# A two-block network on one core: the scan's turns, the last scores of a neighbourhood, and the preparation's products on VectorE

## The chip, the cores and the metric

The program runs on one core of one Trainium2 chip. Its time is the device time in microseconds (us) from start to end of one execution. The engines of the core are TensorE (PE in the profile, its weight loads PEld), VectorE (DVE), ScalarE (ACT), GpSimd (POOL) and SyncE (SP), whose queue issues nearly all the DMAs. Before the change the median of three runs is 4197.6 us, from 4195.8 to 4206.4. The profile was taken in a further execution, of 4200.8 us.

## The reference, cut to what matters

Two blocks follow one another, each of two layers. The change touches the layers of the first block alone. A layer projects 256 context and 1024 latent tokens, runs a recurrence over them in both directions (six heads of 64), a full attention, and a neighbourhood attention, in which a row of 64 queries sees eight rows of keys, with a bias for each place, and all 256 context keys:

```
def _rwkv7_step(S, inp):                  # lax.scan, forwards and backwards
    r, w, k, v, kk, b = inp
    sa = einsum('bhvk,bhk->bhv', S, kk)
    S = S * w - sa[..., None] * b + v[..., None] * k
    return S, einsum('bhvk,bhk->bhv', S, r)

def row_block(r):                         # neighbourhood attention
    s_nb  = einsum('bqhd,bpqjhd->bhqpj', q_r, k_nb) + bias
    s_ctx = einsum('bqhd,bchd->bhqc', q_r, k_ctx)
    p = softmax(concatenate([s_nb, s_ctx], -1))
    return p_nb @ v_nb + p_ctx @ v_ctx
```

Here `kk` is the normalized key, `kd = k * (1 + (iclr - 1) * k_a)` stands for `k` in the step, and `b = kk * iclr`.

## The kernel before, in words

The recurrence is computed in 20 steps of 64 tokens, both directions in one step. Within a step the 64 x 64 triangular system of the recurrence is inverted, so that a step is only matmuls.

**Preparation** (`rwkv_pre`, in `project`) makes what the steps need. For each of the 20 steps `front` loads r, k and kk (`RKK`), forms the decay's running sum `L` with a scan on VectorE (line 869), its exponentials `pf` and `pinv` on ScalarE, the rates `ic` (line 866, GpSimd), `b` (line 876, GpSimd) and `kd` (lines 878 and 879, VectorE), and from these the four products of `T4` (lines 885 to 888, one of them on GpSimd). In the trace `T4` is called `T`. `back` multiplies two of the four on TensorE and stores all of them. After five steps `rwkv_solve` inverts 30 systems at once: a product into `stmp` (`dot`, line 956, in turn on GpSimd and VectorE) and a sum over it (line 958, VectorE), first row by row, then with blocks of 8 and of 16. There are four solves in a layer. All of this is a generator which `project` runs in turn with the remaining projections (`late_proj`, matmuls `pj`). A weight of the projections is split into `hhi` (ScalarE) and the rest `hlo` (`split`, line 129); `lo_engine` says which engine takes the second, and during the preparation that is GpSimd.

**The scan** (`rwkv_steps`) runs after that, in turn with the attention (`attention1`). `seqs` gives turns: the scan has weight 60, the attention 80 (`W1`), so that four turns of the attention go with three of the scan. A step takes three turns: first `rw<-SV,Z` and half of the next step's `fetch` (direction 0: `rw<-T`, masked on VectorE into `Z` and `G`), then `rw<-W,TT`, then `rw<-SV,BT` and `rw<-G,SV`. At its end the rest of `fetch` is drained at once: direction 1's `rw<-T`, and the transposes of both directions, copied to `BT` by ScalarE. The tiles `rw` have three buffers in PSUM. 

**The attention** finds the largest score of every query first (`maxima`). For each tile of 128 queries and each head scores are written to `S` (two buffers) and reduced on VectorE (line 1451). A neighbourhood tile has 512 keys with a bias (`biased`, line 1458), then 256 context keys, and for the tiles 2 to 5 of 8 another 64 keys with a bias, written into the same `S` behind the context's. After that `weights` makes T = scores transposed, exponentials `gP`, and blends `Y`.

TensorE's order is that of the code (`ordered`); a scheduler orders the other engines. Each engine runs its queue in order.

## Time and profile before

| stretch of the span (us) | what runs | length | TensorE busy | VectorE busy | GpSimd busy |
|---|---|---|---|---|---|
| 280 to 690 | preparation, first layer | 410 | 351.3 | 308.1 | 224.0 |
| 690 to 1103 | scan, first layer | 413 | 350.8 | 271.8 | 211.4 |
| 1580 to 2017 | preparation, second layer | 437 | 367.1 | 308.5 | 231.7 |
| 2017 to 2415 | scan, second layer | 398 | 352.1 | 264.8 | 206.6 |
| whole span | both blocks | 4198.9 | 3669.6 | 2750.2 | 1551.5 |

The profiled execution took 4200.8 us, of which 4198.9 are the span in the profile. The first block's scans and preparations are 1658 us of it, the four stretches of the table; the rest is the first projections of each layer, the end of its attention, the output projections and the second block. Busy times of TensorE include the time in which its clock is reduced.

### The profile page before, as it was taken

The page shows a single profiled execution, that of the slowest core. Times are in us where ns is not written, and L with a number is a line of the kernel's source. Part 1 is how long each engine was busy: PE and PEld are TensorE (multiplying, and loading weights), DVE is VectorE, ACT ScalarE, POOL GpSimd, SP SyncE. Part 2 cuts the span into 40 slices and gives each one's busy share as a digit, 9 for nine tenths or more (in the row PEclk, how much of TensorE's full clock was granted, in tenths as well). Part 3 has the DMA queues.
Part 4 walks back from the last instruction along what each step waited for, and adds up shares of the span by engine and source line. Part 5 has one row for each costly group of instructions (what it writes and reads, how often), then busy time and mean ns, then how long its engine had stood idle before and what let it go on. Part 6 is the DMA issues. An engine that isn't in the chain of part 4 may idle for free. (4 is left out here: it accounts for less than half of the span.)

```text
span 4198.9 us, 67804 instructions
## 1 busy us (share of the span) xinstructions
PE 3669.6 (87%) x25828; PEld 2732.5 (65%) x25828; DVE 2750.2 (65%) x4527; ACT 1722.4 (41%) x3354; POOL 1551.5 (37%) x1482
## 2 busy tenths in 40 slices
PE   7999887988888899887888988898889799788988
PEld 5767665655546677665555645686667687566767
DVE  4547877666787755778557677756766553676655
ACT  3235442333442225443334443235555522555551
POOL 2215653555663223556355564103111320311132
PEclk9999988999999999888899999898999999899999
DMA  6448654233334226773423234233232342322233
GB/s 241 167 116 186 156 142 129 89 100 105 120 96 157 81 80 162 169 164 98 136 88 120 82 127 148 92 123 98 67 97 81 102 141 85 103 73 93 75 107 126
DMA packets 509845, 495.75 MB, mean 118 GB/s; under 512 B 296360, under 2 KB 412616, under 8 KB 505168
## 3 DMA queue, kind: packets, MB, share of 16 engines
q1 hardware_dynamic: 469264, 455.76, 36.4%
q10 hardware_dynamic: 40256, 35.66, 2.8%
q8 instruction: 204, 3.34, 0.3%
q14 instruction: 121, 0.99, 0.1%
HBM read 323.81 MB, written 167.49 MB: 117 GB/s over the span
## 5 line engine op out<-in xcount | busy, mean ns | idle before, releaser
L107 PE MATMUL pj<-hthi,hhi 128*128 128x512 f32 (+2 forms) x2120 | 868.6, 410 | 49.7 <-DVE stg L715 31.4
L107 PE MATMUL pj<-hthi,hlo 128*128 128x512 f32 (+2 forms) x2120 | 814.3, 384 | 4.2 <-POOL hlo L129 4.2
L107 PE MATMUL pj<-htlo,hhi 128*128 128x512 f32 (+2 forms) x2120 | 814.6, 384 | 0.5 <-DVE htlo L129 0.5
L107 PEld LDWEIGHTS pj<-hthi,hhi 128*128 128x128 f32 (+1 forms) x2120 | 413.9, 195 | 158.5 <-DVE stg L715 34.0
L107 PEld LDWEIGHTS pj<-hthi,hlo 128*128 128x128 f32 (+1 forms) x2120 | 411.9, 194 | 86.1 <-POOL hlo L129 4.6
L107 PEld LDWEIGHTS pj<-htlo,hhi 128*128 128x128 f32 (+1 forms) x2120 | 414.4, 195 | 61.7 <-DVE htlo L129 1.6
L1544 POOL TENSOR_TENSOR acc<-acc,gP 128x512 f32<-128x512 f32 (+1 forms) x240 | 305.2, 1284 | 173.0 <-ACT gP L1538 155.9
L129 POOL TENSOR_TENSOR hlo<-hraw,hhi 128x1024 fp32r<-128x1024 f32 x65 | 168.9, 2599 | 251.1 <-ACT hhi L128 243.0
L1538 ACT ACTIVATE gP<-T 128x512 f32<-128x512 f32 (+1 forms) x292 | 167.1, 583 | 190.8 <-PE T L107 178.8
L1451 DVE TENSOR_REDUCE gmx<-S 128x1 f32<-128x512 f32 (+1 forms) x372 | 202.5, 555 | 60.2 <-PE S L107 58.2
L107 PE MATMUL po<-who,yh 128*128 128x512 f32 x544 | 216.7, 398 | 27.5 <-ACT yh L1658 22.6
L107 PE MATMUL S<-K,B 128*128 128x512 f32 (+2 forms) x448 | 174.3, 390 | 67.7 <-DVE gmx L1451 59.7
L107 PE MATMUL po<-wlo,yh 128*128 128x512 f32 x544 | 216.2, 397 | 0.0
L107 PE MATMUL po<-who,yl 128*128 128x512 f32 x544 | 214.1, 395 | 1.1 <-POOL yl L1659 1.1
L128 ACT CAST hhi<-hraw 128x1024 fp32r<-128x1024 f32 x118 | 123.8, 1049 | 220.9 <-PE pj L107 178.1
L1182 POOL TENSOR_SCALAR RL<-rl 128x128 f32<-128x128 f32 (+1 forms) x80 | 35.6, 446 | 467.3 <-DVE rl L1299 415.4
L107 PE MATMUL Y<-gP,V 128*64 128x512 f32 (+1 forms) x776 | 202.9, 608 | 2.0 <-DVE ys L1557 2.0
L107 PEld LDWEIGHTS S<-K,B 128*128 128x128 f32 x448 | 86.7, 193 | 153.8 <-DVE gmx L1451 108.2
L107 PE MATMUL T<-B,K 128*128 128x512 f32 (+1 forms) x368 | 167.1, 454 | 11.2 <-ACT gP L1538 9.8
L107 PE MATMUL S<-KL,L 128*128 128x512 f32 (+2 forms) x448 | 158.3, 354 | 0.0
L107 PE MATMUL T<-L,KL 128*128 128x512 f32 (+1 forms) x368 | 145.4, 396 | 2.7 <-DVE L L122 2.7
L1659 POOL TENSOR_TENSOR yl<-yr,yh 128x1024 fp32r<-128x1024 f32 x34 | 83.1, 2443 | 162.1 <-ACT yh L1658 144.9
(422 smaller groups left out, 8499.9 us busy)
## 6 DMA issues: line engine op xcount, KB each, us to landing
hraw<-in_w_in_dram SPq DMA_DIRECT2D x110, 512.0 KB
T<-d_PRE SPq DMA_DIRECT2D x40, 768.0 KB
mw<-in_w_mod_dram SPq DMA_DIRECT2D x24, 1024.0 KB
RKK<-d_U SPq DMA_DIRECT2D x80, 288.0 KB
yr<-d_YT ACTq DMA_DIRECT2D x34, 512.0 KB
d_G<-stg SPq DMA_DIRECT2D x64, 256.0 KB
woraw<-in_w_out_dram SPq DMA_DIRECT2D x32, 512.0 KB
d_PRE<-T SPq DMA_DIRECT2D x40, 384.0 KB
```

Of the source, the lines that this page charges most:

```text
L107: self.nc.tensor.matmul(out, lhsT=lhsT, rhs=rhs, start=start, stop=stop, skip_group_check=True)
L128: self.nc.scalar.copy(hi, src)
L129: self.lo_engine.tensor_tensor(out=lo, in0=src, in1=hi.bitcast(F32), op=ALU.subtract)
L1182: self.nc.gpsimd.tensor_scalar(out=out, in0=in_, scalar1=1.0, scalar2=0.0, op0=ALU.mult, op1=ALU.add)
L1451: nc.vector.tensor_reduce(out=m, in_=S[:, 0:w], op=ALU.max, axis=AX.X, negate=True)
L1538: nc.scalar.activation(P, T, AF.Exp)
L1544: eng.tensor_tensor(out=acc[h][:, cs], in0=acc[h][:, cs], in1=P, op=ALU.add)
L1659: nc.gpsimd.tensor_tensor(out=yl, in0=y, in1=yh.bitcast(F32), op=ALU.subtract)
```

## The change

Five things change. In a neighbourhood tile the scores of the last 64 keys are written together with the context's, ahead of the reduction of these; the two reductions follow. In the scan `fetch` is given out in two parts: the transposes of direction 0 (`turn(0)`) with direction 1's products in a turn of their own, `turn(1)` at the end of the step. A step then has four turns, and with weight 79 against 80 the scan and the attention alternate strictly. In the preparation GpSimd's pieces go to VectorE: `ic`, `b`, the product with r, `hlo`, and GpSimd's half of the solve's products. `b` and `kd` share a tile `BK`, so that their two products with `pinv` are one instruction. And the solve's 16-blocks leave out what a triangular block has as zeros: a product has 1024, 768, 512 and 256 columns instead of four times 1024. The sums over them shrink alike.

```diff
-                    seqs((scan, 60), att, until=scan)
+                    seqs((scan, 79), att, until=scan)
...
-                self.lo_engine = self.nc.gpsimd
...
-                nc.gpsimd.tensor_scalar(out=ic[:, d], in0=th[1][:, d, :, o:o + 64], scalar1=0.5, scalar2=0.5, op0=ALU.mult,
+                nc.vector.tensor_scalar(out=ic[:, d], in0=th[1][:, d, :, o:o + 64], scalar1=0.5, scalar2=0.5, op0=ALU.mult,
                                         op1=ALU.add)
...
-            b = t3("b")
-            nc.gpsimd.tensor_tensor(out=b, in0=ic, in1=kk, op=ALU.mult)
-            kd = t3("kd")
+            BK = self.tl(rp, [128, 2, 2, 3, 64], F32, "BK")
+            kd = BK[:, 1]
+            nc.vector.tensor_tensor(out=BK[:, 0], in0=ic, in1=kk, op=ALU.mult)
...
-                nc.gpsimd.tensor_tensor(out=T4[:, d, :, 1, :], in0=self.rev(r[:, d], d), in1=pf[:, d, :, 1:65], op=ALU.mult)
-                nc.vector.tensor_tensor(out=T4[:, d, :, 2, :], in0=self.rev(b[:, d], d), in1=pinv[:, d], op=ALU.mult)
-                nc.vector.tensor_tensor(out=T4[:, d, :, 3, :], in0=self.rev(kd[:, d], d), in1=pinv[:, d], op=ALU.mult)
+                nc.vector.tensor_tensor(out=T4[:, d, :, 1, :], in0=self.rev(r[:, d], d), in1=pf[:, d, :, 1:65], op=ALU.mult)
+                both = BK[:, :, d, :, ::-1] if d else BK[:, :, d]
+                nc.vector.tensor_tensor(out=T4[:, d, :, 2:4, :].rearrange("p a q t -> p q a t"), in0=both,
+                                        in1=pinv[:, d].unsqueeze(1).to_broadcast([128, 2, 3, 64]), op=ALU.mult)
...
-            self.turn = (self.turn + 1) % 2
-            (nc.gpsimd if self.turn else nc.vector).tensor_tensor(out=tv, in0=x.to_broadcast([128] + shape),
-                                                                  in1=y.to_broadcast([128] + shape), op=ALU.mult)
+            nc.vector.tensor_tensor(out=tv, in0=x.to_broadcast([128] + shape), in1=y.to_broadcast([128] + shape), op=ALU.mult)
...
-                    dot(X[:, i:i + step, :], blk(D, o + n, o, n)[:, i:i + step, :].unsqueeze(2), t11, [step, n, n])
+                    dot(X[:, :, i:i + step], blk(D, o + n, o, n)[:, :, i:].unsqueeze(2), t11[:, i:i + step, i:].unsqueeze(1),
+                        [n, step, n - i])
...
+            def turn(d):
+                ps = self.tl(rpp, [128, 3, 128], F32, "rw", 3)
+                for p in range(3):
+                    self.tr(ps[:, p, :], row(T4[:, d, p, 2:4, :]), self.ID)
+                nc.scalar.copy(BT[:, d], ps)
             for d in range(2):
+                if d:
+                    turn(0)
                 gp = [self.tl(rpp, [128, 3, 128], F32, "rw", 3) for _ in range(2)]
...
-            BT = self.tl(rp, [128, 2, 3, 128], F32, "BT", 2)
-            for d in range(2):
-                ps = self.tl(rpp, [128, 3, 128], F32, "rw", 3)
-                for p in range(3):
-                    self.tr(ps[:, p, :], row(T4[:, d, p, 2:4, :]), self.ID)
-                nc.scalar.copy(BT[:, d], ps)
-            yield
+            turn(1)
             return tok, AR, TT, G, Z, BT
...
             if st < 19:
+                next(ahead)
+                yield
                 ready = self.drain(ahead)
...
                 scores(S[:, 0:w], h, t, k0, w)
+                if near:
+                    scores(S[:, w:w + near[2]], h, t, *near[1:3])
                 m = mx[:, t, 1 - h, c:c + 1]
                 nc.vector.tensor_reduce(out=m, in_=S[:, 0:w], op=ALU.max, axis=AX.X, negate=True)
                 if near:
                     biased(S, w, h, t, *near)
             def biased(S, o, h, t, c, k0, w, b0):
-                scores(S[:, o:o + w], h, t, k0, w)
```

Line 107 before is line 106 after, 110 is 109, and 956 is 953. The instructions' numbers of tiles differ between the two programs.

TensorE before, in the first layer's scan where a step ends and the next begins (`T` is the step's operands, `rw` a PSUM tile, `CST` holds the identity for the transposes):

```order
L107 MATMUL T_7949<-acc_7711,ONES 64x256
L107 MATMUL rw_7959<-T_1261_7742 128x128
L107 MATMUL rw_7960<-T_1261_7742 128x128
...
L110 MATMUL rw_7972<-CST,T_1261_7742 128x128 x3
L110 MATMUL rw_7977<-CST,T_1261_7742 128x128 x3
L107 MATMUL rw_7991<-SV_7741,Z_7766 64x64 x12
L107 MATMUL rw_8008<-T_1318_7983 128x128
```

TensorE after, at the same place:

```order
L106 MATMUL T_7890<-acc_7652,ONES 64x256
L109 MATMUL rw_7900<-CST,T_1245_7698 128x128 x3
L106 MATMUL rw_7905<-T_1245_7698 128x128
L106 MATMUL rw_7906<-T_1245_7698 128x128
...
L106 MATMUL T_7917<-B_6147,K_5963 128x512
...
L106 MATMUL S_7944<-KL_6598,L_6943 128x64
L109 MATMUL rw_7955<-CST,T_1245_7698 128x128 x3
L106 MATMUL rw_7969<-SV_7697,Z_7722 64x64 x12
L106 MATMUL rw_7987<-T_1308_7961 128x128
```

The first three transposes now stand ahead of direction 1's six products, and a turn of the attention stands between these products and the last three transposes with `rw<-SV,Z`.

TensorE before, with what an instruction waits for, at the first neighbourhood tile with 64 more keys (`S` scores, first layer's scan):

```order
L107 MATMUL S_7873<-K_6656,B_7001 128x256 [waits DVE_49]
L107 MATMUL S_7873<-KL_6657,L_7002 128x256
L107 MATMUL S_7873<-K_6656,B_7001 128x64 [waits DVE_49]
L107 MATMUL S_7873<-KL_6657,L_7002 128x64
L107 MATMUL S_7881<-K_6656,B_7001 128x512
```

TensorE after, at the same tile:

```order
L106 MATMUL S_7814<-K_6597,B_6942 128x256 [waits DVE_49]
L106 MATMUL S_7814<-KL_6598,L_6943 128x256
L106 MATMUL S_7814<-K_6597,B_6942 128x64
L106 MATMUL S_7814<-KL_6598,L_6943 128x64
L106 MATMUL S_7822<-K_6597,B_6942 128x512 [waits DVE_49]
```

The wait for VectorE ahead of the 64 keys is gone, and the next tile of scores, which takes the other buffer of `S`, has one.

VectorE after, in the first layer's preparation, near the end of a solve (`BK` holds b and kd, `stmp` a product, `sX` and `sT` blocks of the inverse, `hlo` a weight's rest):

```order
L953 TENSOR_TENSOR stmp_3887<-sT_3417,sX_618_3783 128x256
L953 TENSOR_TENSOR stmp_3902<-sT_3417,sX_618_3783 128x512
L128 TENSOR_TENSOR hlo_3820<-hraw_3817,hhi_3819 128x1024
L954 TENSOR_REDUCE sT_3417<-stmp_3887 128x4x16
L954 TENSOR_REDUCE sT_3417<-stmp_3902 128x4x16
...
L874 TENSOR_TENSOR BK_4006<-ic_3995,RKK_3991 128x384
L875 SCALAR_TENSOR_TENSOR BK_4006<-ic_3995,ka_418_2562 128x384
L953 TENSOR_TENSOR stmp_3915<-sT_3417,sX_618_3783 128x768
L953 TENSOR_TENSOR stmp_3924<-sT_3417,sX_618_3783 128x1024
```

Before, `hlo`, `b` and two of these four products, each of 1024 columns, stood in GpSimd's queue; now all are in VectorE's, between the solve and the steps' own products.

## Rows read from the trace of the kernel before

**Rows 1.** Busy time by stretch: the two preparations and the two scans, with TensorE's granted clock.

```profile
280.00:690.00 410.00, 351.30 (x3005) 285.83 (x3003) 308.12 (x356) 186.12 (x462) 223.97 (x220) 0.91 0.62 150
690.00:1103.00 413.00, 350.76 (x3903) 241.68 (x3902) 271.79 (x615) 159.12 (x318) 211.36 (x224) 0.95 0.33 101
1580.00:2017.00 437.00, 367.11 (x2894) 286.04 (x2892) 308.51 (x368) 190.16 (x463) 231.70 (x214) 0.88 0.62 150
2017.00:2415.00 398.00, 352.13 (x3714) 235.29 (x3714) 264.83 (x591) 154.23 (x294) 206.59 (x211) 0.96 0.33 104
```

**Rows 2.** TensorE's waits, first preparation: us in total, times, longest us.

```profile
PE pre L107 <- ACT sXs L997: 15.7, 8, 7.1
PE pre L107 <- DVE T L887: 15.1, 2, 14.1
PE pj L107 <- DVE stg L706: 9.2, 5, 5.0
```

**Rows 3.** TensorE's longest wait in the second preparation.

```profile
PE pre L107 <- DVE sD L984: 21.4, 2, 19.4
```

**Rows 4.** TensorE's waits, first scan.

```profile
PE S L107 <- DVE gmx L1451: 27.5, 29, 7.5
PE rw L110 <- DVE G L1055: 22.5, 19, 7.1
```

**Rows 5.** TensorE's waits, second scan.

```profile
PE S L107 <- DVE gmx L1451: 18.3, 26, 2.5
PE rw L110 <- DVE G L1055: 12.8, 19, 1.9
```

**Rows 6.** TensorE's timeline: first and last of 32 waits ahead of 64 keys.

```profile
811.15 0.30 PE L107 MATMUL S<-K,B 128*128 128x64 f32 x1 [1.86 <-DVE gmx L1451]
...
2338.47 0.30 PE L107 MATMUL S<-K,B 128*128 128x64 f32 x1 [0.52 <-DVE gmx L1451]
```

**Rows 7.** TensorE's timeline: second group of transposes at the end of a step.

```profile
728.38 0.52 PE L110 MATMUL rw<-CST,T 128*128 128x128 f32 x3 [0.43 <-DVE G L1055]
```

**Rows 8.** Both preparations' busy sums: L956, L958, tiles RKK and pinv, L869, L878.

```profile
sum 847.00, DVE 131.30 POOL 151.02; mean DVE 65.65 POOL 75.51
sum 847.00, DVE 111.16; mean DVE 55.58
sum 847.00, DVE 89.42 POOL 110.17; mean DVE 44.71 POOL 55.08
sum 847.00, DVE 88.21 ACT 20.87; mean DVE 44.11 ACT 10.43
sum 847.00, DVE 54.71; mean DVE 27.35
sum 847.00, DVE 28.74; mean DVE 14.37
```

**Rows 9.** Timeline of VectorE and GpSimd in the first preparation: start, duration.

```profile
540.52 0.96 DVE L869 TENSOR_TENSOR_SCAN L<-rst,lw 128x384 f32<-128x384 f32 x1 [1.93 <-ACT lw L865]
...
555.31 0.35 DVE L885 TENSOR_TENSOR T<-RKK,pPF 128x192 f32<-128x192 f32 x1
...
564.97 2.93 POOL L956 TENSOR_TENSOR stmp<-sD,sT 128x1024 f32<-128x1024 f32 x1 [2.58 <-DVE sT L958]
565.93 2.79 DVE L869 TENSOR_TENSOR_SCAN L<-rst,lw 128x384 f32<-128x384 f32 x1
568.64 2.18 DVE L956 TENSOR_TENSOR stmp<-sD,sT 128x1024 f32<-128x1024 f32 x1
```

**Rows 10.** VectorE's longest wait for GpSimd, first preparation.

```profile
DVE L L869 <- POOL ic L866: 10.9, 1, 10.9
```

**Rows 11.** VectorE's waits for GpSimd's products, second preparation.

```profile
DVE sT L958 <- POOL stmp L956: 9.7, 10, 1.8
```

**Rows 12.** Weight splits on VectorE, whole span: busy, mean ns, idle before and releaser.

```profile
L129 DVE TENSOR_TENSOR hlo<-hraw,hhi 128x1024 fp32r<-128x1024 f32 x53 | 65.4, 1234 | 91.2 <-ACT hhi L128 90.3
```

**Rows 13.** The rates on GpSimd in the second preparation, same columns.

```profile
L866 POOL TENSOR_SCALAR ic<-th 128x192 f32<-128x192 f32 x40 | 23.9, 605 | 75.2 <-ACT th L147 53.7 <-issue 16.6 <-DVE L L869 2.6
```

More of the change, by code (lines that the diff above doesn't have):

```diff
@@ L81, in __init__ @@
         self.flip = 0
-        self.turn = 0
         self.tanhs, self.logs = [], []
@@ L563, in project @@
                     next(att)
-                self.lo_engine = self.nc.vector
                 while self.flow:
@@ L973, in rwkv_solve @@
                 X = self.tl(rp, [128, n, n], F32, f"sX{n}", 2 if n == 8 else 1)
-                t11 = blk(T, o, o, n).rearrange("p j k -> p k j").unsqueeze(1)
+                t11 = blk(T, o, o, n).rearrange("p j k -> p k j")
                 for i in range(0, n, step):
-                    dot(X[:, i:i + step, :], blk(D, o + n, o, n)[:, i:i + step, :].unsqueeze(2), t11, [step, n, n])
+                    dot(X[:, :, i:i + step], blk(D, o + n, o, n)[:, :, i:].unsqueeze(2), t11[:, i:i + step, i:].unsqueeze(1),
+                        [n, step, n - i])
                     yield
-                xv = X.rearrange("p j k -> p k j").unsqueeze(1)
+                xv = X.rearrange("p j k -> p k j")
                 for i in range(0, n, step):
-                    dot(blk(T, o + n, o, n)[:, i:i + step, :], blk(T, o + n, o + n, n)[:, i:i + step, :].unsqueeze(2), xv,
-                        [step, n, n])
+                    j = i + step
+                    dot(blk(T, o + n, o, n)[:, i:j, :], blk(T, o + n, o + n, n)[:, i:j, 0:j].unsqueeze(2), xv[:, :, 0:j].unsqueeze(1),
+                        [step, n, j])
                     yield
@@ L1045, in fetch @@
             Z = self.tl(rp, [128, 2, 2, 3, 64], F32, "Z", 2)
+            BT = self.tl(rp, [128, 2, 3, 128], F32, "BT", 2)
+            def turn(d):
[3 more added lines that the diff above has]
+                nc.scalar.copy(BT[:, d], ps)
             for d in range(2):
+                if d:
+                    turn(0)
                 gp = [self.tl(rpp, [128, 3, 128], F32, "rw", 3) for _ in range(2)]
@@ L1473, in maxima @@
                     b0 = (14 + j0 - 3) * 64 if 2 <= i <= 5 else (j0 - 1) * 64
-                    biased(room("S"), 0, h, t, 0, k0, 512, b0)
+                    S = room("S")
+                    scores(S, h, t, k0, 512)
+                    biased(S, 0, h, t, 0, k0, 512, b0)
                     yield
```

## The prediction, made before the changed kernel had run

> **What bounds the kernel now.** I first cut the span into the stretches that the change touches [rows 1]: in each, TensorE is busy for 351 to 367 us of 398 to 437, and no other engine is busier. TensorE runs in the order of the code, so whatever it waits for there lengthens the span; that is the list to read next. In the preparations the waits are on the chain through VectorE: in the first 15.1 us for the steps' products `T`, 15.7 for `sXs` (ScalarE, the end of a solve) and 9.2 for `stg` [rows 2], in the second 21.4 for the last transposes of a solve [rows 3]. Together 61.4 us. In the scans they are of two kinds: scores waiting for a reduction (27.5 and 18.3 us) and transposes waiting for masks (22.5 and 12.8) [rows 4, 5]. The third thing to see is the clock: 0.91 and 0.88 granted in the preparations, 0.95 and 0.96 in the scans [rows 1]. These are means over stretches at 1.2 and 2.4 GHz.
>
> All terms are made against the profiled execution, whose 4198.9 us of span are 1.9 less than its own 4200.8 us, and 4200.8 is 3.2 above the median of 4197.6. I take the differences from the median.
>
> **Part A, the last 64 scores.** They stand behind a wait for the reduction of the context's scores in the same tile. There are 16 such tiles a layer (tiles 2 to 5, two heads, two pairs of heads), 32 in all; in the trace each has its wait, the first 1.86 us, the last 0.52 [rows 6], and 0.52 is also the smallest. This is reduction plus signal, with VectorE at leisure. The change takes the wait from the order; the next tile then waits for the other buffer of `S`, whose reduction stands earlier in VectorE's queue. So I count 0.52 for each as gone, 32 x 0.52 = 16.6 us, and leave what is above that, VectorE being late, where it is: it will stand at the next tile. The bounds are 0 (all of it moves to the next tile) and the 45.8 us of all waits of that line [rows 4, 5], which can't all go. The reduction itself now starts after 64 more keys are scored; VectorE is busy for 272 of 413 us there, and hides it. I take **-17**.
>
> **Part B, the turns of the scan.** The second group of transposes takes the PSUM buffer that VectorE's masks of the same half step still read: 0.43 us at the least [rows 7], 35.3 us in 38 waits, at worst 7.1 [rows 4, 5]. After the change a buffer comes free a turn of the attention earlier. `turn(0)` takes the one that ScalarE's copies of `Yt` release, `turn(1)` the one of `turn(0)`; both releases have a turn between. The transposes, 12 products and copies are as many as before, and the attention's turns as well (80 in 79 instead of 80 in 60), so no work moves out of the scan. What it costs: between `rw<-SV,Z` and `rw<-W,TT`, and between that and `rw<-SV,BT`, there is now one attention turn, where there were one or two. ScalarE's queue, with its exponentials, stands in the first of these chains. Direction 0's next products also want the buffer that the copy of `turn(1)` leaves, with `rw<-SV,Z` as cover. At 0.43 in a quarter of 38 steps that is 4 us; at 0.43 in all, twice a step, 33, and the part is worth nothing. The first fetch of each scan is drained whole and keeps its wait. I take 35.3 less 4, less some 6 for the long waits that have another cause behind them: **-25**, from 0 to -35.
>
> **Part C, the preparation.** GpSimd gives up `ic`, `b`, one product, `hlo` and half of the solve's products. First the price on VectorE. A scan of 384 columns takes 0.96 us by itself, but 2.79 where it starts inside GpSimd's 2.93 us product, and it ends when that has ended plus its own time [rows 9]: the two engines don't overlap there. So the means of now are stretched, and I price with the undisturbed rows: 0.35 for 192 columns, 0.96 for the scan, 2.18 for a product of 1024 [rows 9], 1.23 for `hlo` [rows 12]; from 0.35 and 1.23, 1.06 ns for a column, so 0.55 for 384. VectorE now, both layers [rows 8]: products 131.3, sums 111.2, lines 885 and 879 89.4, lines 887 and 888 88.2, scan 54.7, line 878 28.7: 503.5 us. After:
> products of a solve, blocks of 16: twice (1024+768+512+256) columns, 5 x 2.18 = 10.9; blocks of 8: 4 x 1.09 = 4.4; seven small ones at no more than 0.35, 2.5; eight solves, 142. Sums by their columns, 7728 for 10800 a solve: 79.5. 160 pieces of 192, 56, and lines 879, 876 and 878 in 40 steps at 0.55, 66. The 80 joint products, 44. 80 `ic`, at most 0.35 each, 28. 40 scans, 38.4. 31 `hlo`, 38.1. Sum 492: **12 us less** than now. VectorE takes all of GpSimd's work and isn't fuller for it, as the 16-blocks shrink and nothing stretches it. Second, its waits for GpSimd go: 10.9 for `ic` [rows 10] and 9.7 for products [rows 11], 20.6. Where VectorE bounds, the stretch shortens by these 33 us; TensorE's 61.4 us of waits there [rows 2, 3] are room enough, and the end nearest to it in kind. Bounds: -61 if all of these go; for the other end, what the moved pieces bring with them. `hlo` on VectorE waits 90.3 / 53 = 1.70 us for ScalarE's `hhi` elsewhere [rows 12]; 31 of them would be 53, which makes +20. In a full queue `hhi` is ready long before, so I take **-33**. `b` and `kd` now share one buffer, whose store must be out before the next `b`; the store stood ahead of the next `kd` before, one place later, so I cost that at nothing.
>
> The stretched scan [rows 9] is what the Trainium skill states in SBUF — State Buffer, section Who interferes with whom: a VectorE instruction with two SBUF inputs and a GpSimd instruction that reads SBUF block each other, and the second waits for the whole of the first. The trace agrees (2.79 for 0.96). If it were a slowing of VectorE for another reason, part C would be worth nothing. Against the change speaks Perfetto Trace Analysis of the Trainium skill, Optimizing Scalar/DVE Operations: with a saturated VectorE, giving work to ScalarE or even GpSimd may make sense, though between VectorE and GpSimd it might not help. By the first half of this sentence, moving the work back is a loss, the third rival below.
>
> **Part D, the clock.** It is lower where TensorE has waited. One hundredth of the preparations' 718 us busy [rows 1] is 7 us. With half of the waits gone I take **-5**, from 0 to -30 (the preparations at the scans' clock).
>
> Sum: -17 - 25 - 33 - 5 = -80, 4197.6 - 80 = 4117.6, or **4118 us**.
>
> **The rivals.**
> *One half only.* Either the scans keep their time, since a released wait turns up at the next instruction, or the preparations do, since VectorE's work is nearly what it was. For it: 492 against 503.5 is hardly a relief. Against: the waits of parts A and B are each tied to an order that is gone. -42 or -38: 4155 to 4160, in all 4148 to 4178.
> *The preparations become TensorE's alone.* Once no product hangs on GpSimd, the fronts finish early, ScalarE is no longer held by them, and the 61 us and most of the clock go: -17 - 25 - 61 - 25 = -128, 4070.
> *VectorE's queue becomes the bound, slower.* VectorE runs in order; every moved piece brings the wait that it had on GpSimd: 31 `hlo` at 1.70, 53 us, and `ic`, which waited 75.2 us in the second preparation, 53.7 of it for ScalarE's `th` [rows 13]. Twice 53.7 and 53 are 160; less 33 and the scans' 42 that is +85, 4283; at half of these waits +5. It decides once more than 88 of the 160 us fall on VectorE. Against it: the scan `L` waits for the same pair `th` in VectorE's queue already, and `ic` stands next to it.
> *The change doesn't do what it says:* TensorE's time isn't set by these waits, as the transfers or ScalarE stand behind them: within 12.6 us of before.
>
> **How the numbers follow.** A measurement of this kernel can tell about 0.3% from no change, 12.6 us. Forecast, 4088 to 4148: 0.43. One half only: 0.23. TensorE's alone, under 4088: 0.18, a third of it under 4060. Nothing: 0.09. Slower: 0.07. Faster by over 0.3% are the first three: 0.84; same 0.09; slower 0.07. The range leaves out the lowest third of the third case, nothing and slower, and a little above 4178: **4060 to 4180**, about 0.78.
>
> **What would show it.** Right for A: no wait ahead of a 64-key score, and the waits of `S` for line 1451 down by some 17 us. For B: under 10 us of transposes waiting in both scans. For C: VectorE's busy time of the preparations within 20 us of now, products of 1024 columns near 2.2 us and scans near 0.96, GpSimd's busy time there down by over half, and the 14.1 and 19.4 us waits shortened. For D: a granted clock of 0.92 or more in both. I am wrong if VectorE's idle time ahead of `hlo` or `ic` is over 80 us, if the products cost far above 2.18 us for 1024 columns, or if waits of TensorE for `SV`, `W` or `BT` fill what A and B give.

## The result, and the profile after

The changed kernel takes 4051.1 us in the median of four executions (4044.2 to 4058.5); the kernel before, run beside it, 4202.0. The ratio is 0.9645, with a 95% interval from 0.9616 to 0.9675: some 149 us less. The forecast was 4118 with a range from 4060 to 4180. The direction was right, the size was not: the gain is 1.9 times the one forecast, and the time lies 9 us below the range.

The profiled execution has a span of 4051.1 us, 147.8 less than that of before. I cut both spans at the same events: the first `rw<-T` and the last `rw<-G,SV` of each scan, the first load of `yr`, and the first product `pre<-T` of the second preparation.

| stretch | before | after | difference |
|---|---|---|---|
| first preparation (280 to the first scan) | 408.0 | 369.0 | -39.0 |
| first scan | 412.1 | 379.3 | -32.8 |
| end of the first layer's attention | 180.9 | 179.1 | -1.8 |
| second layer's first projections | 352.6 | 353.9 | +1.3 |
| second preparation, from its first product | 384.1 | 334.6 | -49.5 |
| second scan | 395.0 | 367.3 | -27.7 |
| all that follows | 1786.2 | 1787.9 | +1.7 |

So the gain lies where the change was made and nowhere else: 88.5 us in the preparations, where 38 were forecast, and 60.5 in the scans, where 42 were forecast.

Busy time by stretch after the change, the lines that answer to [rows 1] (stretch, its length, then TensorE, weight loads, VectorE, ScalarE, GpSimd with their counts; granted clock, DMA share, GB/s):

```profile
280.00:649.00 369.00, 340.10 (x2993) 277.05 (x2991) 277.91 (x468) 184.84 (x460) 33.11 (x67) 0.96 0.68 166
649.00:1028.30 379.30, 343.35 (x3901) 241.05 (x3902) 266.90 (x611) 157.89 (x316) 207.87 (x222) 0.95 0.36 109
...
1507.70:1895.90 388.20, 347.24 (x2895) 271.63 (x2893) 293.47 (x481) 189.94 (x465) 33.46 (x58) 0.94 0.70 170
1895.90:2263.20 367.30, 341.36 (x3704) 233.88 (x3706) 265.88 (x588) 151.33 (x290) 207.97 (x213) 0.96 0.35 111
```

Three things are to be seen. GpSimd's busy time in the preparations has fallen from 224 and 232 us to 33 and 33. VectorE, which took its work over, is busy for less and not for more: 277.9 for 308.1, and 293.5 for 308.5. And TensorE, with the same matmuls, is busy for 340.1 where it was 351.3, and for 347.2 where it was 367.1, at a granted clock of 0.96 and 0.94 where it was 0.91 and 0.88.

TensorE's waits after, first in the first preparation, then in the second (engine and line, what it waited for: us in total, times, longest), for [rows 2, 3]:

```profile
PE pre L106 <- DVE sD L983: 8.9, 1, 8.9
PE pj L106 <- DVE stg L703: 7.5, 4, 5.5
PE pre L106 <- ACT sXs L996: 5.3, 8, 2.1
...
PE pre L106 <- DVE T L885: 1.4, 1, 1.4
...
PE pre L106 <- DVE sD L983: 14.0, 2, 10.2
```

The wait of 15.1 us for `T` is down to 1.4, `sXs` from 15.7 to 5.3, the 21.4 us of `sD` in the second preparation to 14.0. All of TensorE's idle time in the two preparations (length less busy, the second from its first product) falls from 128.5 to 69.1 us, by 59.4, its busy time by 29.1.

The same list for the two scans, for [rows 4, 5]:

```profile
PE S L106 <- DVE gmx L1458: 16.8, 14, 6.0
PE S L106 <- DVE gmx L1464: 6.3, 5, 3.2
PE rw L106 <- DVE G L1064: 4.1, 2, 3.3
...
PE S L106 <- DVE gmx L1458: 10.2, 12, 4.2
PE S L106 <- DVE gmx L1464: 4.0, 1, 4.0
```

Line 1458 is line 1451 of before: 27.0 us for 45.8. Line 1464, 1458 before, has 10.3 us for 2.7, so that a part of what went stands at the next reduction. No wait of a transpose for `G` is left, where there were 35.3 us. TensorE's timeline after, at a tile with 64 more keys and at the end of a step (start, duration), for [rows 6, 7]:

```profile
766.68 0.28 PE L106 MATMUL S<-K,B 128*128 128x256 f32 x1
766.80 0.28 PE L106 MATMUL S<-KL,L 128*128 128x256 f32 x1
766.92 0.19 PE L106 MATMUL S<-K,B 128*128 128x64 f32 x1
766.95 0.27 PE L106 MATMUL S<-KL,L 128*128 128x64 f32 x1
...
790.50 0.55 PE L109 MATMUL rw<-CST,T 128*128 128x128 f32 x3
790.98 0.94 PE L106 MATMUL rw<-T 64*128 64x128 f32 x12
...
794.10 0.55 PE L109 MATMUL rw<-CST,T 128*128 128x128 f32 x3
```

The 64 keys follow the context's 0.12 us later with no wait, and neither group of transposes has one.

### The profile page after: what moved, and what is told of

It reads as the page before. It is cut to its first block, busy times and chain, and to the rows that moved or that the text cites. A ratio compares the mean times of both kernels' runs of the same rounds, so it can differ in the third digit from the quotient of the medians.

```text
span 4051.1 us, 67400 instructions
## 1 busy us (share of the span) xinstructions
PE 3626.5 (90%) x25828; PEld 2711.8 (67%) x25828; DVE 2703.0 (67%) x4754; ACT 1717.4 (42%) x3354; POOL 1166.1 (29%) x1175
## 5 line engine op out<-in xcount | busy, mean ns | idle before, releaser
L106 PE MATMUL pj<-hthi,hhi 128*128 128x512 f32 (+2 forms) x2120 | 862.2, 407 | 46.5 <-DVE stg L712 30.9
L128 DVE TENSOR_TENSOR hlo<-hraw,hhi 128x1024 fp32r<-128x1024 f32 x84 | 104.6, 1246 | 103.3 <-ACT hhi L127 102.5
L128 POOL TENSOR_TENSOR hlo<-hraw,hhi 128x1024 fp32r<-128x1024 f32 x34 | 88.0, 2590 | 228.1 <-ACT hhi L127 221.1
```

The source lines that it names most:

```text
L106: self.nc.tensor.matmul(out, lhsT=lhsT, rhs=rhs, start=start, stop=stop, skip_group_check=True)
L128: self.lo_engine.tensor_tensor(out=lo, in0=src, in1=hi.bitcast(F32), op=ALU.subtract)
```

## The experiments

The first runs take the change apart: each makes a part of it, or two, on the kernel before.

**Part A alone.**

```diff
                 scores(S[:, 0:w], h, t, k0, w)
+                if near:
+                    scores(S[:, w:w + near[2]], h, t, *near[1:3])
...
             def biased(S, o, h, t, c, k0, w, b0):
-                scores(S[:, o:o + w], h, t, k0, w)
...
```

> Before with part A alone (the last 64 scores written with the context's). Theory (each part takes away its own waits, and the two scans' 60.5 us are the sum of A and B): 32 waits of at least 0.52 us go, about -17 us, at most -25 with the clock, so 4177 to 4185 for 4202; the wait ahead of a 64-key score is gone and the waits of S for VectorE in the two scans fall from 48.5 to some 30 us. Rival (the wait moves to the next tile's buffer of S, and only the strict turns gave the scans their time): within 6 us of before, with as many us of waits of S as before.

Measured: 0.9901 (0.9866 to 0.9936), 4161.6 us beside 4205.7. The scans took 398.3 and 387.9 us, 20.9 less than before. Waits in the first and then in the second scan:

```profile
PE rw L110 <- DVE G L1055: 23.1, 19, 7.1
PE S L107 <- DVE gmx L1453: 14.8, 13, 7.4
...
PE rw L110 <- DVE G L1055: 15.4, 20, 1.9
PE S L107 <- DVE gmx L1453: 9.1, 9, 5.7
```

The waits of line 1453 (1451 before) fell from 45.8 to 23.9, and the transposes wait no less than before (38.5 us for 35.3). So A is worth what its own waits say, 21 us where 17 were forecast. The other half of its 42 us has no place in A: the second preparation took 368.6 us where it had taken 384.1, though no line of it differs.

**Part B alone.**

```diff
-                    seqs((scan, 60), att, until=scan)
+                    seqs((scan, 79), att, until=scan)
...
             for d in range(2):
+                if d:
+                    turn(0)
...
+                next(ahead)
+                yield
                 ready = self.drain(ahead)
```

> Before with part B alone (fetch in two parts, strict turns 79 to 80). Theory: the 35.3 us of transposes that wait for G go, and some clock with them: -35 to -45 us, 4157 to 4167 for 4202; transposes wait under 1 us. Rival (B is most of the scans' gain, A next to nothing): -52 to -60 us. Second rival (without A the freed time falls into the waits ahead of the 64 keys): under -25 us, and the waits of S for VectorE in the scans above 55 us.

Measured: 0.9894 (0.9864 to 0.9924). The scans took 397.1 and 389.1, again 20.9 us less, and the second preparation 367.2. The scores' waits, first and second scan:

```profile
PE S L107 <- DVE gmx L1457: 34.1, 30, 8.2
...
PE S L107 <- DVE gmx L1457: 32.5, 28, 12.4
```

The transposes' 35.3 us are gone, and the scores for line 1457 (1451) wait 66.6 us where they waited 45.8. So 20.8 us of waiting turn up at the scores as long as A isn't there.

**Parts A and B together,** without C.

```diff
-                    seqs((scan, 60), att, until=scan)
+                    seqs((scan, 79), att, until=scan)
...
+                if near:
+                    scores(S[:, w:w + near[2]], h, t, *near[1:3])
...
+                if d:
+                    turn(0)
```

> Before with parts A and B, the preparation as it was. A alone gave the two scans 20.9 us, B alone 20.9 (and its S waits for VectorE grew by 21 us), the whole change 60.5. Theory (B alone moves waits of transposes to the 64-key scores, A alone leaves the transposes; only together do both go): the scans shorten by 55 to 62 us, and with 15 us of the second preparation the time is 4122 to 4135 for 4202. Rival (a part of the scans' 60.5 came from the preparation that ended sooner and left the chip in another state of its clock): the scans shorten by 40 to 46 us, 4140 to 4150.

Measured: 0.9859 (0.9826 to 0.9892). The scans took 379.3 and 375.0 us, 52.8 less: more than the 41.8 of A and B apart, so that B is worth 32 us once A is there, but 8 less than with all of the change. The second preparation took 370.7. The first scan is as long as with all of the change (379.3), so those 8 us are all in the second. They stand at its start, where the attention's scores wait for a reduction on VectorE; TensorE's timeline of A and B without C, in the two layers:

```profile
715.71 0.58 PE L107 MATMUL S<-K,B 128*128 128x256 f32 x1 [9.98 <-DVE gmx L1459]
...
1997.83 0.58 PE L107 MATMUL S<-K,B 128*128 128x256 f32 x1 [12.35 <-DVE gmx L1459]
```

and of the changed kernel:

```profile
672.65 0.58 PE L106 MATMUL S<-K,B 128*128 128x256 f32 x1 [5.97 <-DVE gmx L1458]
...
1918.49 0.50 PE L106 MATMUL S<-K,B 128*128 128x512 f32 x1 [4.17 <-DVE gmx L1458]
```

That is 4.0 and 8.2 us less; in the first layer's scan TensorE is busy for 2.7 us more against it. The reduction stands in VectorE's queue behind a piece of the attention's keys, and VectorE waits there for ScalarE (10.30 and 11.97 us of idle time, in the changed kernel 6.29 and 3.72), which itself waits for the load of these keys (15.73 and 17.40, in the changed kernel 11.72 and 10.50). The changed kernel with its 16-blocks whole, below, is like A and B alone in this: 16.08 us for the load in the second layer, and scans of 380.1 and 373.9 us, 754.0 in all for 754.3. The runs below that keep the smaller blocks and the weight of 79 have 738.8 to 749.8. So the 8 us go with the smaller blocks; why the load comes sooner behind them was not followed up.

**The kernel before once more,** without any edit, to see how firm its second preparation is.

> The kernel before once more, unchanged, for its stretches. With part A or part B alone the second preparation, in which neither changes a line, took 368.6 and 367.2 us from its first product of steps, and 384.1 in the profile of before. Theory (the scheduler has put GpSimd's and SP's queues of that preparation in another order there, and that is worth 15 us): 382 to 386 us again, with a wait of over 4 us for ScalarE's sXs and one for GpSimd's hlo. Rival (one execution of before was late there by chance): 367 to 378 us.

Measured: one execution of 4193.4 us, its second preparation 378.0 us, the first 407.4, the scans 412.2 and 394.7. So 6 of the 15 us lie between two executions of one program, and 378.0 is the upper end of what the rival expected; the three kernels that change nothing there took 367.2 to 370.7, 7 to 11 us below this execution. The scheduler does put a few instructions of GpSimd and SP in another order there (an `hlo` two places later, loads of `RKK` ahead of stores); whether that is the cause stays open.

**Part C alone.**

```diff
-                self.lo_engine = self.nc.gpsimd
...
-                nc.gpsimd.tensor_scalar(out=ic[:, d], in0=th[1][:, d, :, o:o + 64], scalar1=0.5, scalar2=0.5, op0=ALU.mult,
+                nc.vector.tensor_scalar(out=ic[:, d], in0=th[1][:, d, :, o:o + 64], scalar1=0.5, scalar2=0.5, op0=ALU.mult,
...
-                    dot(X[:, i:i + step, :], blk(D, o + n, o, n)[:, i:i + step, :].unsqueeze(2), t11, [step, n, n])
+                    dot(X[:, :, i:i + step], blk(D, o + n, o, n)[:, :, i:].unsqueeze(2), t11[:, i:i + step, i:].unsqueeze(1),
+                        [n, step, n - i])
```

> Before with part C alone (the preparation's pieces on VectorE, joint product, smaller 16-blocks). Theory (the preparations' 88.5 us come from C alone, waits and clock together): -80 to -95 us, 4107 to 4122 for 4202, with a granted clock of 0.94 to 0.96 in both preparations and scans of 412 and 395 us as before. Rival (the clock's part of it came from the whole program's denser run, not from C): -55 to -65 us, clock 0.92 or less in the preparations.

Measured: 0.976 (0.9729 to 0.979). The preparations took 371.1 and 331.6 us, as in the changed kernel (369.0 and 334.6), at a clock of 0.95 and 0.94; the scans 410.5 and 396.4, as before. So the preparations' gain is C's, clock included.

**The smaller 16-blocks alone,** all else of the preparation as before.

```diff
-                    dot(X[:, i:i + step, :], blk(D, o + n, o, n)[:, i:i + step, :].unsqueeze(2), t11, [step, n, n])
+                    dot(X[:, :, i:i + step], blk(D, o + n, o, n)[:, :, i:].unsqueeze(2), t11[:, i:i + step, i:].unsqueeze(1),
+                        [n, step, n - i])
...
-                    dot(blk(T, o + n, o, n)[:, i:i + step, :], blk(T, o + n, o + n, n)[:, i:i + step, :].unsqueeze(2), xv,
-                        [step, n, n])
+                    dot(blk(T, o + n, o, n)[:, i:j, :], blk(T, o + n, o + n, n)[:, i:j, 0:j].unsqueeze(2), xv[:, :, 0:j].unsqueeze(1),
+                        [step, n, j])
```

> Before with the smaller 16-blocks of the solves alone; the products still alternate between GpSimd and VectorE, and all else of the preparation stays on GpSimd. Theory (the gain of C is that the two engines no longer hold each other up): at most -20 us, 4182 or more for 4202, with scans L stretched to over 2 us still present. Rival (the gain of C is the 16-blocks' 1536 fewer columns of product and as many of sum in each half): -40 to -60 us, 4142 to 4162.

Measured: 0.9812 (0.9784 to 0.9841), 4127.5 us: 79 of part C's 101. This is where the theory of then, that C is about the two engines holding each other up, fell.

**The 16-blocks whole again,** the rest of the change kept: the last diff the other way round.

```diff
-                    dot(X[:, :, i:i + step], blk(D, o + n, o, n)[:, :, i:].unsqueeze(2), t11[:, i:i + step, i:].unsqueeze(1),
-                        [n, step, n - i])
+                    dot(X[:, i:i + step, :], blk(D, o + n, o, n)[:, i:i + step, :].unsqueeze(2), t11, [step, n, n])
```

> After with the 16-blocks of the solves whole again (four products of 1024 columns and four sums of 1024 on either side of a solve, all on VectorE); the rest of the change is kept. The smaller blocks alone gave before 79 us. Theory (the preparation follows VectorE's queue, and 8 solves lose 3072 columns of product and 3072 of sum each): VectorE busy 80 to 95 us more in the preparations, and the time 45 to 80 us above after, 4096 to 4131. Rival (it was GpSimd's products that held the queue, and with these gone the columns are hidden): within 20 us of after.

Measured: 0.9799 (0.9771 to 0.9826), 1.54% or some 65 us above the change; in the profiles the preparations are 52.3 us longer and the scans 7.4. Against A and B alone (0.9859) it is 25 us faster, though VectorE is busy for 21 us more: the moves alone, without smaller blocks, do bring something.

**The solves' products in turn on both engines again.**

```diff
-            nc.vector.tensor_tensor(out=tv, in0=x.to_broadcast([128] + shape), in1=y.to_broadcast([128] + shape), op=ALU.mult)
+            self.turn = (self.turn + 1) % 2
+            (nc.gpsimd if self.turn else nc.vector).tensor_tensor(out=tv, in0=x.to_broadcast([128] + shape),
+                                                                  in1=y.to_broadcast([128] + shape), op=ALU.mult)
```

> After with the solves' products again in turn on GpSimd and VectorE, blocks small. Theory (a product takes longer on GpSimd and stands in VectorE's way, but the column count decides): 8 to 25 us above after, 4059 to 4076, scans L stretched to over 2 us in a few steps, VectorE's waits for GpSimd's stmp at 5 to 10 us a preparation. Rival (VectorE is the queue that bounds, so half of the products off it help): 5 to 15 us below after. Third (hidden): within 5 us.

Measured: 0.9666 (0.965 to 0.9682), which can't be told from the change.

**`hlo` on GpSimd again.**

```diff
+                self.lo_engine = self.nc.gpsimd
...
```

> After with the weights' rest hlo on GpSimd during the preparation. Smaller 16-blocks made 50 to 79 us of part C, the solves' products on VectorE none, so 20 to 30 us are left for hlo and the steps' pieces. Theory (GpSimd takes 2.4 us for an hlo and VectorE 1.25, and a projection of TensorE waits for it; but VectorE loses 38 us of work): within 12 us of after. Rival (hlo is what carries the rest): 15 to 30 us above after, with waits of pj for GpSimd's hlo on TensorE. Second rival (VectorE's queue bounds): 8 to 20 us below after.

Measured: 0.968 (0.9661 to 0.9698), 10 to 15 us above the change, at the edge of what these intervals tell; its preparations are 16.6 us longer in the profile. A weight's rest of 2.46 us on GpSimd, and VectorE's product of 512 columns that starts 0.34 us behind it (the same product undisturbed is the first row):

```profile
538.93 1.11 DVE L955 TENSOR_TENSOR stmp<-sD,sT 128x512 f32<-128x512 f32 x1
...
548.28 2.46 POOL L128 TENSOR_TENSOR hlo<-hraw,hhi 128x1024 fp32r<-128x1024 f32 x1 [1.55 <-ACT hhi L127]
...
548.62 3.08 DVE L955 TENSOR_TENSOR stmp<-sD,sT 128x512 f32<-128x512 f32 x1
```

**The steps' pieces on GpSimd again.**

```diff
-                nc.vector.tensor_scalar(out=ic[:, d], in0=th[1][:, d, :, o:o + 64], scalar1=0.5, scalar2=0.5, op0=ALU.mult,
+                nc.gpsimd.tensor_scalar(out=ic[:, d], in0=th[1][:, d, :, o:o + 64], scalar1=0.5, scalar2=0.5, op0=ALU.mult,
...
-            nc.vector.tensor_tensor(out=BK[:, 0], in0=ic, in1=kk, op=ALU.mult)
+            nc.gpsimd.tensor_tensor(out=BK[:, 0], in0=ic, in1=kk, op=ALU.mult)
...
-                nc.vector.tensor_tensor(out=T4[:, d, :, 1, :], in0=self.rev(r[:, d], d), in1=pf[:, d, :, 1:65], op=ALU.mult)
+                nc.gpsimd.tensor_tensor(out=T4[:, d, :, 1, :], in0=self.rev(r[:, d], d), in1=pf[:, d, :, 1:65], op=ALU.mult)
```

> After with ic, b and the product with r on GpSimd (the joint product stays on VectorE, hlo too). Theory (these stand in each step's chain from th to T, and each hand-over to GpSimd and back lengthens it): 12 to 30 us above after, with VectorE's waits for GpSimd back at 5 us or more a preparation. Rival (hidden, as the solves' products are): within 6 us. Second rival (VectorE's queue bounds, and 75 us of work less help): 8 to 20 us below after.

Measured: 0.9627 (0.96 to 0.9655), not to be told from the change, if anything below it.

**Both of these groups on GpSimd again,** with `hlo` and the joint product left on VectorE: the last diff and that of the solves' products.

```diff
+            (nc.gpsimd if self.turn else nc.vector).tensor_tensor(out=tv, in0=x.to_broadcast([128] + shape),
+                                                                  in1=y.to_broadcast([128] + shape), op=ALU.mult)
...
+            nc.gpsimd.tensor_tensor(out=BK[:, 0], in0=ic, in1=kk, op=ALU.mult)
```

> After with all that part C moved, but hlo, on GpSimd again: half of the solves' products, ic, b and the product with r; the 16-blocks stay small, the joint product and hlo stay on VectorE. Each of the two groups alone made no difference that could be told (solves' products 0.9666, steps' pieces 0.9627 of before, after 0.9645). Theory (in this preparation an instruction off VectorE's queue saves its time and costs about as much in waiting for GpSimd): within 12 us of after, VectorE busy some 35 us less in the preparations and idle as much more. Rival (the two groups together bring GpSimd back to the load that it had, and with it the old waits): 15 to 35 us above after.

The changed kernel beside it on the same chip, without an edit:

> After once more, unchanged, beside the three kernels that follow, so that these stand against it on one chip. Expected: a ratio to before of 0.962 to 0.967, with preparations of 365 to 372 us and 331 to 338 us (from the first product of steps).

Measured: 4053.3 us and 0.9659 (0.9632 to 0.9686), beside 4053.4 and 0.9657 (0.9629 to 0.9685). What moves_back puts back on GpSimd is worth nothing on VectorE that these runs could tell, alone or together. The sums over both preparations show how; a row is the length of the two stretches and each engine's busy time in them. With both groups back on GpSimd:

```profile
sum 706.60, PE 643.02 PEld 518.11 DVE 517.47 ACT 352.91 POOL 327.22; mean PE 321.51 PEld 259.05 DVE 258.73 ACT 176.45 POOL 163.61
```

The changed kernel:

```profile
sum 703.60, PE 634.54 PEld 511.58 DVE 541.99 ACT 352.64 POOL 63.90; mean PE 317.27 PEld 255.79 DVE 271.00 ACT 176.32 POOL 31.95
```

The kernel before:

```profile
sum 792.10, PE 663.62 PEld 532.98 DVE 588.41 ACT 354.21 POOL 442.37; mean PE 331.81 PEld 266.49 DVE 294.20 ACT 177.11 POOL 221.19
```

And the smaller 16-blocks alone:

```profile
sum 729.20, PE 643.91 PEld 517.82 DVE 519.05 ACT 352.29 POOL 387.69; mean PE 321.95 PEld 258.91 DVE 259.52 ACT 176.15 POOL 193.84
```

GpSimd's 263 us less in the changed kernel cost VectorE 24.5 us of busy time and gave it back 27.5 us of idle time (706.6 less 517.5 is 189.1; 703.6 less 542.0 is 161.6). From before to the smaller blocks alone it is the other way: VectorE's busy time falls by 69.4 us, its idle time stays (203.7 and 210.1), and the stretches shorten by 62.9.

**`b` and `kd` in tiles of their own,** with two products for each direction again, for the step that was costed at nothing.

```diff
-            BK = self.tl(rp, [128, 2, 2, 3, 64], F32, "BK")
-            kd = BK[:, 1]
+            b = t3("b")
+            kd = t3("kd")
...
+                nc.vector.tensor_tensor(out=T4[:, d, :, 2, :], in0=self.rev(b[:, d], d), in1=pinv[:, d], op=ALU.mult)
+                nc.vector.tensor_tensor(out=T4[:, d, :, 3, :], in0=self.rev(kd[:, d], d), in1=pinv[:, d], op=ALU.mult)
```

> After with b and kd in tiles of their own again and two products with pinv for each direction instead of the joint one. In after VectorE waits 23 us in the two preparations for the stores of kd before it can write the next b, 8 us in before. Theory (those waits are on the queue that bounds): VectorE's waits for d_KD fall by some 15 us, its products with pinv take 4 to 6 us more, and the time is 4 to 12 us below after. Rival (other work of VectorE or of TensorE fills the waits): 0 to 8 us above after.

Measured: 0.963 (0.9603 to 0.9657), 8 us below the change beside it, within the intervals. VectorE's waits for that store, first and second preparation:

```profile
DVE kd L875 <- DMA d_KD<-kd: 6.5, 3, 3.1
...
DVE kd L875 <- DMA d_KD<-kd: 12.1, 6, 4.7
```

18.6 us, where the changed kernel has 23.3 in its first profile and 16.9 in the one beside this run. So the waits don't hang on the shared tile. They were 8.2 us in before; that they grew as the steps follow one another faster is likely, but no run shows it.

**Weight 60 for the scan,** `fetch` still in two parts.

```diff
-                    seqs((scan, 79), att, until=scan)
+                    seqs((scan, 60), att, until=scan)
```

> After with weight 60 for the scan instead of 79: fetch still in two parts, so a step has four turns and 5.3 turns of the attention beside it. Theory (the gain of part B is that the transposes stand a turn after their masks, not the weight): the scans get longer by the attention that moves into them, the tail shorter by as much, and the sum changes by under 10 us. Rival (the strict alternation carries it): 15 to 35 us above after, with waits of rw for VectorE of over 15 us in the scans.

Measured: 0.9796 (0.9774 to 0.9818), some 60 us above the change: the rival, but not by its mechanism, since no `rw` waits in the scans for more than 2 us. The first layer's scan and what follows it:

```profile
649.10:1105.50 456.40, 415.79 (x4216) 281.38 (x4218) 326.96 (x714) 191.57 (x377) 256.17 (x263) 0.94 0.31 97
1105.50:1238.10 132.60, 82.59 (x332) 44.34 (x326) 83.77 (x129) 52.11 (x102) 69.09 (x56) 0.79 0.52 164
```

The scan has grown by 77.1 us, the end of the layer shrunk by only 46.5. There TensorE is now busy for 82.6 of 132.6 us at a clock of 0.79, while in the changed kernel it was 153.1 of 179.1: the attention that went into the scan is missing as cover of the recurrence's output, for which TensorE waits 20.2 us there (`oyb` and `oy`), and 0.9 in the changed kernel. So the weight belongs to the four turns: it keeps as much attention behind the scan as before.

**The 8-blocks cut likewise.**

```diff
-            step = min(n, 4 if n == 16 else 8)
+            step = 4
```

> After with the 8-blocks of the solves cut in the same way: 256 and 128 columns in two products for one of 512, four times in a solve, no more yields than before. Theory (the time follows the columns that VectorE works through: 3072 columns of product and of sum a solve were worth some 65 us; here 512 of either go, for four products and four sums more with their fixed cost of 0.06 to 0.15 us): 0 to 8 us below after. Rival (the fixed costs and the longer chain eat it): 0 to 8 us above.

Measured: 0.9632 (0.9609 to 0.9654), about 5 us below the change, within the intervals, with VectorE busy for 8 us less in the preparations.

**The steps' pieces on GpSimd and the 8-blocks cut,** together.

```diff
-            step = min(n, 4 if n == 16 else 8)
+            step = 4
...
-            nc.vector.tensor_tensor(out=BK[:, 0], in0=ic, in1=kk, op=ALU.mult)
+            nc.gpsimd.tensor_tensor(out=BK[:, 0], in0=ic, in1=kk, op=ALU.mult)
...
```

> After with the steps' pieces ic, b and the product with r on GpSimd, and with the 8-blocks of the solves cut as the 16-blocks are: the two variants that came out lowest. Theory (the two gains, some 7 and 5 us by their ratios, add): 8 to 20 us below after. Rival (one of the two was noise): within 7 us of after.

Measured: 4039.1 us, 0.9623 (0.9594 to 0.9651), 14 us below the changed kernel beside it, clearly faster than before; against the change the two intervals still overlap. It is no lower than either edit alone (0.9627 and 0.9632), so that a sum of the two isn't shown.

## Why the prediction was right in direction and too small

**Part A: right.** Forecast 17, alone 21: the waits of 0.52 us each, and some of what lay above them.

**Part B: near alone by luck, low in company.** Forecast 25; 20.9 alone, 32 on top of A. The forecast took 4 us off for new waits and 6 for long waits with another cause; in the run no transpose waits for `G`, and 20.8 us came back at the scores instead. So the prediction took as a sum what isn't one: B alone hands waits to the scores, and A takes these away. Beside the 45.5 us by which TensorE's idle time in the scans fell (42 were forecast) stand 15 us of its busy time, for which the sum had no term: part D was made for the preparations alone.

**Part C: the sum right, its meaning wrong.** The step that failed is the balance for VectorE, "492 against 503.5", and the 20.6 us of waits beside it. The sum itself came out: the instructions that it listed last 487.6 us after the change. Sums and shrunk products were priced well too:

```profile
sum 757.20, DVE 134.32; mean DVE 67.16
...
sum 757.20, DVE 84.88; mean DVE 42.44
```

(products, 142 forecast, and sums, 79.5 forecast, both preparations.) What failed is what the sum was taken for. First, durations added up are not the time of a queue. Neighbours on VectorE that don't need one another overlap; its timeline after:

```profile
522.96 0.55 DVE L874 TENSOR_TENSOR BK<-ic,RKK 128x384 f32<-128x384 f32 x1
523.43 0.55 DVE L875 SCALAR_TENSOR_TENSOR BK<-ic,ka 128x384 f32<-128x384 f32 x1
523.90 0.18 DVE L954 TENSOR_REDUCE sT<-stmp 128x12 f32<-128x36 f32 x1
```

The first two last 0.55 us each, and the next starts 0.47 later. VectorE's busy time falls by 45 us (616.6 to 571.4 over the stretches of [rows 1] and of after), not by 12: the recorded durations of all its instructions there fall by 24 (647.9 to 624.2), and what they overlap grows by 21 (31.3 to 52.8), as the change puts many short instructions side by side. By the prediction's own sign, a busy time within 20 us of now, C was wrong here. Second, VectorE's idle time in these stretches falls by 45 us (230.4 to 185.8), not by 20.6. The 20.6 took one row from each preparation; all of VectorE's direct waits for GpSimd come to 37.4 us, and none is left. The largest wait of all, the scan `L` for ScalarE's `lw`, had no term and fell from 73.3 to 35.3 us; why `lw` comes sooner no run shows by itself. VectorE's waits before, two stretches:

```profile
DVE L L869 <- ACT lw L865: 22.7, 6, 9.4
DVE sT L958 <- POOL stmp L956: 4.3, 8, 0.8
DVE sX L958 <- POOL stmp L956: 3.3, 2, 1.7
...
DVE L L869 <- ACT lw L865: 50.6, 10, 13.8
DVE sX L958 <- POOL stmp L956: 4.1, 3, 1.8
```

and after:

```profile
DVE L L866 <- ACT lw L862: 17.3, 4, 7.5
...
DVE L L866 <- ACT lw L862: 18.0, 7, 6.9
```

New waits, for `th`, `hhi` and the store of `kd`, took a part of that back. Busy and idle time only divide the gain, and TensorE's divide it otherwise (29.1 and 59.4); which edit made it is what the runs show. So third, the prediction let the moved work eat the gain of the smaller blocks, a net of 12. The runs show that moved work to be about free in both directions, and the smaller blocks to carry most: 65 of C's 90 us (against A and B alone), or 79 of 101 (against the kernel before). `hlo` may carry some 10 to 15, and what is left can't be told apart. Whether the blocks' columns count as load of VectorE's queue or as length of the solve's chain, a product and a sum after each other, no run separates: 24.5 us of VectorE's busy time given to GpSimd shortened nothing, but GpSimd's products are in that chain too. That the moves are about free agrees with the half of the sentence that the Trainium skill has in Perfetto Trace Analysis, Optimizing Scalar/DVE Operations, on work between VectorE and GpSimd: it might not help. The product of 3.08 us above is what the Trainium skill describes in SBUF — State Buffer, Who interferes with whom. The trace agrees: it ends 0.96 us after GpSimd's `hlo`, and takes 1.11 undisturbed.

**The step at no cost** (one tile for `b` and `kd`): right as far as the run with tiles of their own can tell.

**Part D: mis-sized.** Forecast 5, with 30 as the end; TensorE's busy time fell by 29.1 us in the preparations and by 15.0 in the scans, the granted clock of the preparations rose to 0.96 and 0.94. In all runs with part C's smaller blocks busy time in the first preparation is 338.6 to 344.0, in all without them 343.4 to 353.9. That shorter waits raise the clock is read from this; no run changed the clock by itself. In the scans it hardly moved (0.95 and 0.96 before as after), so that their 15.0 us have no shown cause.

**The rivals.** The case that came in is the second, the preparations near to TensorE's own time: it named 61 us of waits and 25 of clock, and 59.4 and 29.1 were measured, though 69 us of idle time are left. It had 0.18, and it gave 4070 because it kept 42 us for the scans; with their 60.5 it gives 4051. That it meets the time so closely is luck in part: its reason was that no product hangs on GpSimd any more, and with these products and the steps' pieces back on GpSimd the time is the same. The rival of VectorE's queue, slower, rested on waits that would come along with `hlo` and `ic`: in the changed kernel VectorE waits 16.0 us for `th` ahead of `ic` in the first preparation and 15.0 in the second, and 9.2 and 9.7 ahead of `hlo`, 50 us in all, with less idle time than before.

**The range.** The case at its low end took the bound of C and nearly that of D with the middle of A and B. The bounds of all four lay on one side of the middle and could fall together, as they did.

## What to carry to other kernels

Take a compound edit apart in the prediction, and price each piece as if it were made alone: here fewer columns in products and sums were worth 65 to 79 us, and the moves between engines, which the words of the change put first, nearly nothing beside them, but for what `hlo` may carry. Price a queue by start to start of its instructions and not by their recorded lengths, and let a wait that goes on the engine that bounds bring its share of the clock. Two waits on one path are one term: what the first releases stands at the second until that goes too.

## What the runs showed of the hardware

Two VectorE instructions in a row that don't depend on one another overlap by some 0.08 us in the rows above (0.55 recorded, 0.47 from start to start). 139 us of VectorE's instructions (half of the products' 134.3, and lines 863, 874 and 883 with 24.3, 21.0 and 26.8 in the two preparations) given to GpSimd took only 24.5 us from VectorE's busy time: the recorded durations of what VectorE kept rose by some 90 us, and what they overlap shrank. `hlo` on GpSimd, 37.0 us less to do for VectorE, left it busy for 4.6 us more (546.6 for 542.0). One stretch of one program, the second preparation of the kernel before, took 384.1 us in one execution and 378.0 in another, while the first preparation and both scans agreed within 0.6.
